# First layer's attention: casts of turned weights and turns of rows later in the lists, one root for four blocks, sums in other bursts

## The chip, the cores and the metric

The program runs on one core of a Trainium2 chip. Its engines work side by side, each from a queue of its own that it takes in order: TensorE (PE: products of matrices; its loads of the stationary operand are listed as PEld), VectorE (DVE), ScalarE (ACT), GpSimd (POOL) and SyncE (SP), from which most transfers (DMA) are issued. Semaphores hold an instruction back until what it needs is there. The metric is the time of one execution in microseconds (us); for the kernel before it is the median of three runs.

## The reference, cut to what matters

A trunk of two layers over 512 positions of width 2048, in float32. The first layer is differential attention with eight heads, the second a forgetting attention with sixteen. The change is in the first:

```python
def block(args):                       # 128 queries
    sc = jnp.einsum('bqhcd,bkhcd->bhcqk', qb, k).astype(f32) + bias[None, :, None]
    sc = jnp.where(dist >= 0, sc, NEG)
    p = jax.nn.softmax(sc, axis=-1)
    a = p[:, :, 0] - lam * p[:, :, 1]
    return jnp.einsum('bhqk,bkhe->bqhe', a.astype(v.dtype), v)
o = rms_norm(o, subln_g) * (1.0 - lam_init)
o = o.reshape(B, S, A_WIDTH) * jax.nn.silu(g)
return o @ w_out
```

Each head has two pairs of query and key (width 128), one value and one gate (width 256). Beside this, every layer needs rows of modulation, `c_act @ w_mod[l] + b_mod[l]`: a vector times a matrix of 2048 rows.

## The kernel before, in words

**Products.** Every float32 operand is split in a high part (rounded, by ACT) and a low part (the difference, by DVE), and a product is three products of parts: `products` (L172) issues L174, L175 and L176. A projection is a `group` (L303): four banks of PSUM, one per block of 128, gather sixteen slices of the contraction, two per sub-block. What PE does for one bank and one sub-block, six products, is a burst; a group has 32 of them, numbered from 0. The banks of a group are the same four as those of the group before, so burst 0 of the next group waits until bank 0 has been evacuated, burst 3 until bank 3 has. Weights come through `WeightStream` (L51): SP issues the reads (L47) three sub-blocks ahead into four stages, ACT rounds (L94) and DVE makes the low part (L95) two sub-blocks ahead of PE.

**Lists.** After each burst `tick` (L287) takes one entry of a list `pieces`: a small piece of another task, several pieces, or nothing. Then it runs `bg` steps of a background task. So the entries are places in time, one burst apart. From what is issued in this order a planner makes each engine's queue; where it reckons that an operation is not ready yet it may put a later one ahead. The operations of the background sums are kept in program order.

**Heads.** For heads h = 3 to 7 (L932) there are two groups: `qk[h]`, queries and keys, and `vg[h]`, value and gate. Beside them runs the attention of head h-1: the list `first` beside `qk[h]` (after four entries of nothing, or of the evacuation of head 2), and `rest` beside `vg[h]`. Both groups empty their list before the first evacuation. The evacuation `evac_qk` (L670) rounds (ACT) and makes the low part (DVE, L677 for queries). `evac_vg` (L683) splits v (L169, L170), takes a tanh of the gate (L694) and multiplies (sg, L695). Attention of heads 0, 1 and 7 goes by other lists, `steps` (L864); heads 0 and 1 beside `qk[2]` and `vg[2]`, head 7 beside the first group of the output projection.

**One head by blocks i = 0 to 3 of 128 queries.** `score(i, c)` multiplies (sc), takes the minimum (L723), the exponential (ACT, L727), and for the second of the pair mixes both (L731 to L735). `turn_small(i)` transposes 32 by 32 on DVE and writes to DRAM; `send(i)` issues four transfers that bring it back turned (L767); `take(i)` casts it to high and low parts (ah L777, al L778). `values(i)` multiplies with v (o). After blocks 1 and 3 `norm(p)` (L796) handles the pair p: ACT copies o to `og` and sums the squares (L804); DVE scales (L805), finds the inverse root by `rsqrt` (L242; twelve small operations, L247 to L249 and three rounds of L254 to L256), and multiplies two blocks by root and gate (L808). `turn_og(p)` transposes the rows (L821) and writes them to DRAM (L825), and `fetch` brings them back turned as `ogT` (L833).

**Pools.** `kpool` has sixteen tiles of 128 x 512. It holds the heads' turned rows (two per head) until the output projection's operands are made of them, in the bursts of `vg[7]` (`split_og`, L902: ogs L909, hh L913, hl L914).

**Sums.** `mod_stream` (L354) makes the rows of modulation in the background: DVE multiplies a slice of 128 rows and 512 columns by its part of c and adds (macc, L391). A read (L367) brings two slices, and there are two buffers (`ms`). After sixteen slices the sum is turned, reduced and put through PE (L419, L420, L429). `bg` says after which bursts a step is made: in `qk[h]` by `k % 3 > 0`, in `vg[h]` by `k % 4 > 0`, in the first group of the output projection after every burst, until none is left.

Of the kernel before, what the change touches and what calls it, by code (L numbers as in the profile page):

```python
# [10 lines left out]
F32 = mybir.dt.float32  # L11
F32R = mybir.dt.float32r
I32 = mybir.dt.int32
AF = mybir.ActivationFunctionType
ALU = mybir.AluOpType

P = 128
D = 2048
KT = D // P
T = 512  # L20
TB = T // P
A_HEADS = 8
B_HEADS = 16
NEG = -1e30
EPS = 1e-5
# [85 lines left out]
def tile_yoco(  # L111
# [24 lines left out]
    V, S, PE, G = nc.vector, nc.scalar, nc.tensor, nc.gpsimd  # L136
# [8 lines left out]
    kpool = ctx.enter_context(tc.tile_pool(name="kpool", bufs=16))  # L145
# [95 lines left out]

    def rsqrt(y, v, n, pool):  # L242

        t = pool.tile([P, n], I32, name="rs_t", tag=f"rs_t{n}", bufs=2)
        a = pool.tile([P, n], F32, name="rs_a", tag=f"rs_a{n}", bufs=2)
        h = pool.tile([P, n], F32, name="rs_h", tag=f"rs_h{n}", bufs=2)
        V.tensor_scalar(t, v.bitcast(I32), 1, None, op0=ALU.logical_shift_right)  # L247
        V.tensor_scalar(y.bitcast(I32), t, -1.0, float(0x5F3759DF), op0=ALU.mult, op1=ALU.add)
        V.tensor_scalar(h, v, -0.5, None, op0=ALU.mult)  # L249
        for _ in range(3):  # L250
            if n == 1:
                V.scalar_tensor_tensor(a, y, h, y, op0=ALU.mult, op1=ALU.mult)
            else:
                V.tensor_tensor(a, y, y, op=ALU.mult)  # L254
                V.tensor_tensor(a, a, h, op=ALU.mult)
            V.scalar_tensor_tensor(y, a, 1.5, y, op0=ALU.add, op1=ALU.mult)  # L256
# [182 lines left out]
    with tc.tile_pool(name="start", bufs=2, reuse_waits="tile") as sp, tc.manual_schedule(engines={ET.DVE}):  # L439
# [154 lines left out]
        def turn():  # L594
            lower()
            columns()
            while sum(sets[at["set"] - 1]) <= at["kt"]:
                sums()
                columns()
            turned.append((at["kt"], turn_x(at["kt"])))  # L600
            at["kt"] += 1
# [66 lines left out]
    cur = {}  # L668
# [29 lines left out]
    fetches = {}  # L698

    def attention_a(h, lead=3, late=(), spread=False):  # L700
# [37 lines left out]
        def turn(i):  # L738
            def fn():
                w = (i + 1) * P  # L740
                pt = tr_bank()
                a = st["e", i, 0]
                for j in range(i + 1):
                    PE.transpose(pt[:, j * P : (j + 1) * P], a[:, j * P : (j + 1) * P], ident)
                ah = ap.tile([P, 512], F32R, name="ah", tag="ah")
                al = ap.tile([P, 512], F32R, name="al", tag="al")
                split(ah[:, :w], al[:, :w], pt[:, :w])
                st["a", i] = (ah, al)
            return fn
# [32 lines left out]
        def values(i):  # L782
            def fn():
                if i % 2 == 0:
                    st["o", i // 2] = o_bank()
                o = st["o", i // 2][:, (i % 2) * 256 : (i % 2 + 1) * 256]
                ah, al = st["a", i]
                vh, vl = cur[h, "v"]
                for j in range(i + 1):
                    js = slice(j * P, (j + 1) * P)  # L790
                    products(o, (ah[:, js], al[:, js]), (vh[:, j, :], vl[:, j, :]), j == 0, j == i)
                if i % 2 == 1:
                    norm(i // 2)
            return fn

        def norm(p):  # L796
            o = st["o", p]
            og = ap.tile([P, 2, 256], F32, name="og", tag="og", bufs=1)
            ss = ap.tile([P, 2], F32, name="ss", tag="ss", bufs=2)
            rstd = ap.tile([P, 2], F32, name="rstd", tag="rstd", bufs=2)  # L800
            S.copy(og.rearrange("p r e -> p (r e)"), o)
            for r in range(2):
                orow = o[:, r * 256 : (r + 1) * 256]
                S.activation(orow, orow, AF.Square, accum_out=ss[:, r : r + 1])  # L804
            V.tensor_scalar(ss, ss, 1.0 / 256.0, EPS, op0=ALU.mult, op1=ALU.add)  # L805
            rsqrt(rstd, ss, 2, ap)
            for r in range(2):
                V.scalar_tensor_tensor(  # L808
                    og[:, r, :], og[:, r, :], rstd[:, r : r + 1], cur[h, "sg"][:, 2 * p + r, :],
                    op0=ALU.mult, op1=ALU.mult,  # L810
                )
            st["og", p] = og

        def turn_og(p):
            def fn():
                if p == 0:
                    st["turned"] = dram.tile([P, TB * 256], F32, name="turned_og", tag="turned_og", bufs=2)
                t = ap.tile([P, 512], F32, name="tog", tag="tog", bufs=1)  # L820
                V.transpose(  # L821
                    t.rearrange("p (b r c) -> p r b c", r=2, c=32), st["og", p].rearrange("p r (b c) -> p r b c", c=32)
                )
                to = st["turned"].rearrange("p (b t c) -> p b t c", t=TB, c=32)[:, :, 2 * p : 2 * p + 2, :]
                nc.sync.dma_start(to, t.rearrange("p (b r c) -> p b r c", r=2, c=32))  # L825
            return fn
# [23 lines left out]
        if spread:  # L850
            r, d, k = ([part(i) for i in range(TB)] for part in (turn_small, send, take))
            first = [
                score(0, 0), None, score(0, 1), None, [score(1, 0), r[0]], None, [score(1, 1), d[0]], None, [k[0], r[1]], None,
                [score(2, 0), d[1]], values(0), k[1], None, score(2, 1), None, [values(1), r[2]], score(3, 0), d[2], None, k[2],
                score(3, 1),
            ]
            rest = [
                values(2), r[3], turn_og(0), d[3], None, k[3], None, None, None, values(3), *[None] * 9, turn_og(1), None, None,
                None, fetch,
            ]  # L860
            if h == 2:
                first[9] = fetches[1]
            return first, rest
        steps = [  # L864
            *[None] * lead, score(0, 0), *late[0:1], score(0, 1), *late[1:2], score(1, 0), *late[2:3], score(1, 1), *late[3:4],
# [6 lines left out]
        if h == A_HEADS - 1:  # L872
# [1 line left out]
                values(2), store(0), turn(3), store(1), values(3), None, None, None, None, store(2), store(3),  # L874
            ]
        return steps + [
            values(2), turn_og(0), turn(3), None, values(3), None, None, None, None, turn_og(1), None,
        ]

    def drain():  # L880
# [51 lines left out]
    for h in range(3, A_HEADS):  # L932

        first_steps, rest = attention_a(h - 1, spread=True)
        if h == 3:
            pieces.extend(lambda b=b: evac_qk(2)(b, raw["qk", b]) for b in range(4))
            late = first_vg(2, raw)
            for n in range(4):
                first_steps[2 * n + 1] = late[n]
        else:  # L940
            pieces.extend([None] * 4)
        pieces.extend(first_steps)

        def evac(b, acc, h=h):
            if b == 0:
                drain()
            evac_qk(h)(b, acc)

        group(qk[h], False, evac, bg=lambda k: k % 3 > 0)
        pieces.extend(rest)  # L950

        def evac_rest(b, acc, h=h):
            if b == 0:
                drain()
            evac_vg(h)(b, acc)

        def early(s):
            if s >= 1:
                split_og((2 * s - 2, 2 * s - 1))

        group(vg[h], True, evac_rest, bg=lambda k: k % 4 > 0, after_sub=early if h == A_HEADS - 1 else None)

    def ktile(name):
        return kpool.tile([P, T], F32, name=name, tag="K")
# [14 lines left out]
    def out_projection(jobs, layer, zp, opened, residual, norm, after_held=None):  # L979


        ready = {}

        def prepare(k):
            if k < len(jobs):
                ready[k] = residual(jobs[k][0], jobs[k][2])

        prepare(0)
        for k, (f, job, banks) in enumerate(jobs):
            if layer == 1:  # L990

                pieces.extend([None] * (8 if k else 0) + [lambda k=k: prepare(k + 1)])
            elif k:
                prepare(k)
            res = ready[k]
            gate = ktile("gate")
            row_bcast(gate, gate_dram[layer][0, 512 * f : 512 * (f + 1)])

            def evac(b, acc, f=f, res=res, gate=gate):
                if f == 0 and b == 0:  # L1000
                    drain()
                    opened()
                pool, z, stats = zp
                zs = z[:, b, 512 * f : 512 * (f + 1)]
                tmp = pool.tile([P, 512], F32, name="ztmp", tag="htmp", bufs=2)
                V.tensor_tensor(tmp, acc, gate, op=ALU.mult)
                res(b, zs, tmp)
                V.bn_stats(stats[:, b, f, :], zs)
                if f == 3:
                    norm(b)  # L1010

            last = k == len(jobs) - 1
            group(job, True, evac, banks, bg=1 if k == 0 and layer == 0 else 0, hold=(5, 6)[layer] if last else 0, after_held=after_held if last else None)

    nctx = ExitStack()
    zp = []
# [475 lines left out]
```

## Time and profile before

| what | before |
|---|---|
| median of 3 runs | 1970.86 us (1968.74 to 1971.88) |
| the profiled execution | 1972.9 us, of it 1970.8 in its span |
| PE busy | 1928.8 us, 98% |
| PEld busy | 1596.6 us, 81% |
| DVE busy | 1351.6 us, 69% |
| ACT busy | 695.6 us, 35% |
| granted clock of PE, mean | 0.994 |

The groups of the first layer lie, by the trace, between about 180 and 816 us; the output projection follows. In a row of the timeline stand the start (us), the duration, the engine, the line, the operation, what is written and read, and in brackets the idle time of the engine ahead of it with what ended that. A row of waits gives who waited for whom, the total, how often, and the longest. A row of windows gives for a stretch of time what each engine was busy for, the granted clock, the DMA engines' share and their rate. PE's products are pipelined, so that the next starts before the one ahead has ended as drawn.

### The profile page before, as it was taken

What the parts mean: (1) busy time and instruction counts of PE and PEld (TensorE: products, weight loads), DVE (VectorE), ACT (ScalarE), POOL (GpSimd) and SP (SyncE); (2) the same over time, 40 slices, a digit from 0 to 9 for tenths busy, and PEclk for the clock granted to TensorE, in tenths of its full rate; (3) what the DMA queues carried; (4) which work ended last, traced back from release to release, by engine and by line L of the source; (5) the groups of instructions that cost most, each with busy time, mean ns of one, the idle gap of its engine ahead of it and who ended that gap; (6) DMA issues with size and microseconds to landing.
All of it is one profiled execution on the core that took longest, in us unless ns stands there. A gap on an engine that the chain in (4) does not pass through costs nothing.

```text
span 1970.8 us, 25187 instructions
## 1 busy us (share of the span) xinstructions
PE 1928.8 (98%) x8833; PEld 1596.6 (81%) x8833; DVE 1351.6 (69%) x2494; ACT 695.6 (35%) x1175; POOL 2.2 (0%) x10
## 2 busy tenths in 40 slices
PE   5999999999999999999999999999999999999997
PEld 4888888788888878788888888888888888888886
DVE  7885678777777778853475665666466666676657
ACT  2432444323333334431264222224344344353123
POOL 0000000000000000000000000000000000000000
PEclk8999999999999999999999999999999999999999
DMA  9983455777777777753345765664355555553622
GB/s 343 356 306 111 129 177 168 233 228 221 248 229 241 225 242 222 235 169 97 108 160 193 261 230 193 224 219 134 110 149 152 156 152 158 148 172 114 229 88 106
DMA packets 336378, 376.11 MB, mean 191 GB/s; under 512 B 69334, under 2 KB 238316, under 8 KB 335484
## 3 DMA queue, kind: packets, MB, share of 16 engines
q1 hardware_dynamic: 333872, 370.30, 59.3%
q10 hardware_dynamic: 2380, 4.21, 0.6%
q8 instruction: 69, 1.13, 0.2%
q14 instruction: 57, 0.47, 0.1%
HBM read 345.63 MB, written 28.79 MB: 190 GB/s over the span
## 4 chain that ended last, share of the span: by engine, by line
PE 83%; DVE 8%; DMA 6%; issue 1%; SPq 1%; ACT 1%; DVEq 0%; ACTq 0%
PE acc L174 24%; PE acc L175 24%; PE acc L176 24%; DMA ms<-in_w_mod_dram 2%; DVE macc L391 2%; DMA ms<-in_kv_w_mod_dram 2%; PE sc L174 2%; PE sc L175 2%; PE sc L176 2%; PE o L174 1%; DVE wlo L95 1%; PE o L176 1%; PE o L175 1%; SPq L471 1%; DMA sms<-in_w_mod_dram 1%
## 5 line engine op out<-in xcount | busy, mean ns | idle before, releaser
L95 DVE TENSOR_TENSOR wlo<-wst,whi 128x1024 fp32r<-128x1024 f32 (+2 forms) x322 | 384.3, 1195 | 338.7 <-ACT whi L94 329.4
L94 ACT CAST whi<-wst 128x1024 fp32r<-128x1024 f32 (+2 forms) x322 | 331.6, 1031 | 755.9 <-PE acc L176 361.8
L174 PE MATMUL acc<-whi,hh 128*128 128x512 f32 x1232 | 482.5, 395 | 5.3 <-DVE sg L695 2.4
L175 PE MATMUL acc<-wlo,hh 128*128 128x512 f32 x1232 | 480.9, 390 | 0.3 <-DVE wlo L95 0.3
L176 PE MATMUL acc<-whi,hl 128*128 128x512 f32 x1232 | 480.5, 390 | 0.0
L174 PE MATMUL acc<-hh,whi 128*128 128x512 f32 x1184 | 463.5, 391 | 1.2 <-DVE sg L695 1.1
L175 PE MATMUL acc<-hl,whi 128*128 128x512 f32 x1184 | 461.6, 390 | 0.0
L176 PE MATMUL acc<-hh,wlo 128*128 128x512 f32 x1184 | 461.2, 389 | 0.0
L174 PEld LDWEIGHTS acc<-whi,hh 128*128 128x128 f32 x1232 | 232.7, 189 | 54.3 <-issue 4.6
L176 PEld LDWEIGHTS acc<-whi,hl 128*128 128x128 f32 x1232 | 231.7, 188 | 48.6
L175 PEld LDWEIGHTS acc<-wlo,hh 128*128 128x128 f32 x1232 | 231.9, 188 | 46.4 <-DVE wlo L95 0.7
L176 PEld LDWEIGHTS acc<-hh,wlo 128*128 128x128 f32 x1184 | 222.3, 188 | 47.5
L174 PEld LDWEIGHTS acc<-hh,whi 128*128 128x128 f32 x1184 | 222.5, 188 | 45.3 <-issue 1.9
L175 PEld LDWEIGHTS acc<-hl,whi 128*128 128x128 f32 x1184 | 222.6, 188 | 42.0
L391 DVE SCALAR_TENSOR_TENSOR macc<-ms,cact,macc 128x512 f32<-128x512 f32 x300 | 223.7, 746 | 42.5 <-DMA ms<-in_kv_w_mod_dram 24.7
L498 DVE SCALAR_TENSOR_TENSOR sacc<-sms,cact,sacc 128x512 f32<-128x512 f32 (+1 forms) x127 | 89.5, 705 | 4.8 <-DMA sms<-in_w_mod_dram 1.2
L727 ACT ACTIVATE e<-e,mn 128x128 f32<-128x128 f32 (+3 forms) x64 | 36.0, 563 | 112.1 <-DVE mn L723 108.5
L1298 ACT ACTIVATE eb<-eb,mnb 128x128 f32<-128x128 f32 (+1 forms) x64 | 36.0, 563 | 89.1 <-DVE mnb L1295 88.9
L1295 DVE CUSTOM_DVE_ANT_0 eb<-sc,biasb 128x128 f32<-128x128 f32 (+1 forms) x64 | 31.1, 486 | 22.4 <-PE sc L176 21.6
L391 DVE SCALAR_TENSOR_TENSOR macc<-msk,cact,macc 128x512 f32<-128x512 f32 x60 | 45.0, 750 | 1.4
L723 DVE CUSTOM_DVE_ANT_0 e<-sc,bias 128x128 f32<-128x128 f32 (+3 forms) x64 | 30.9, 484 | 16.7 <-PE sc L176 16.5
L1289 DVE SCALAR_TENSOR_TENSOR biasb<-nfb,F,mask 128x128 f32<-128x128 f32 (+1 forms) x64 | 34.7, 543 | 0.6
(270 smaller groups left out, 1734.3 us busy)
## 6 DMA issues: line engine op xcount, KB each, us to landing
wst<-in_a_w_in_dram SPq DMA_DIRECT2D x240, 256.0 KB, 4.1
ms<-in_w_mod_dram SPq DMA_DIRECT2D x64, 512.0 KB, 4.4
ms<-in_kv_w_mod_dram SPq DMA_DIRECT2D x64, 512.0 KB, 4.7
wst<-in_kv_w_dram SPq DMA_DIRECT2D x64, 512.0 KB, 3.8
wst<-in_b_w_in_dram SPq DMA_DIRECT2D x128, 256.0 KB, 3.0
sms<-in_w_mod_dram SPq DMA_DIRECT2D x56, 512.0 KB, 6.8
wst<-in_a_w_out_dram SPq DMA_DIRECT2D x32, 512.0 KB, 3.8
msk<-in_w_mod_dram SPq DMA_DIRECT2D x64, 256.0 KB, 5.8
```

Source lines behind the costliest of these rows:

```text
L94: self.nc.scalar.copy(hi[:, :, :w], st[:, :, :w])
L95: self.nc.vector.tensor_tensor(lo[:, :, :w], st[:, :, :w], hi[:, :, :w].bitcast(F32), op=ALU.subtract)
L174: PE.matmul(dst, lhs[0], rhs[0], start=start, stop=False)
L175: PE.matmul(dst, lhs[0], rhs[1], start=False, stop=False)
L176: PE.matmul(dst, lhs[1], rhs[0], start=False, stop=stop)
L391: ins = V.scalar_tensor_tensor(acc, w, cact[:, kt : kt + 1], acc, op0=ALU.mult, op1=ALU.add)
L498: V.scalar_tensor_tensor(acc, w, sc, acc, op0=ALU.mult, op1=ALU.add)
L723: V.tensor_tensor_reduce(out=e[:, :w], in0=sc[:, :w], in1=st["bias"][:, (3 - i) * P :], scale=-1.0, scalar=3.0e38, op0=ALU.add, op1=ALU.mi ...
L727: S.activation(e[:, :w], e[:, :w], AF.Exp, bias=mn, scale=-1.0, accum_out=rs)
L1289: V.scalar_tensor_tensor(bias[:, :w], cur[hd, "nf"][:, :w], F[:, i, hd : hd + 1], mask[:, (3 - i) * P :], op0=ALU.add, op1=ALU.add)
L1295: V.tensor_tensor_reduce(out=e[:, :w], in0=sc[:, :w], in1=bias[:, :w], scale=-1.0, scalar=3.0e38, op0=ALU.add, op1=ALU.min, accum_out=mn)
L1298: S.activation(e[:, :w], e[:, :w], AF.Exp, bias=mn, scale=-1.0, accum_out=rs)
```

## The change

Four things, all in the first layer's attention:

- *Lists.* In `first` the casts of blocks 0, 1 and 2 stand one entry later (from 8, 12 and 20 to 9, 13 and 21). In `rest` the cast of block 3 goes from entry 5 to 7, the value products of block 3 from 9 to 11, the turn of the first two blocks' rows from 2 to 17; the turn of the other two stays at 19 and the fetch at 23. In the lists of heads 0 and 1 the first turn of rows goes next to the second.
- *One root.* For all heads but the last, `norm(0)` only copies and sums the squares, into a tile of four columns; `norm(1)` finds the root of four columns at once and scales all four blocks. The second pair's copy and its turned rows lie in tiles of `kpool`. The last head keeps a root for each pair.
- *Sums.* In `qk[h]` steps follow bursts under 26 that leave less than 4 on division by 5 (21 steps, as before). In `vg[h]` they follow bursts under 28 that are no multiple of 7 (24 steps, as before); in `vg[7]` the bound is 24 (20 steps). In the first group of the output projection they begin after burst 4.
- *Tiles of `rsqrt`.* They are four columns wide whatever is asked for, and are cut to it.

```diff
     def rsqrt(y, v, n, pool):
 
-        t = pool.tile([P, n], I32, name="rs_t", tag=f"rs_t{n}", bufs=2)
-        a = pool.tile([P, n], F32, name="rs_a", tag=f"rs_a{n}", bufs=2)
-        h = pool.tile([P, n], F32, name="rs_h", tag=f"rs_h{n}", bufs=2)
+        t, a, h = (pool.tile([P, 4], d, name=k, tag=k, bufs=2)[:, :n] for k, d in (("rs_t", I32), ("rs_a", F32), ("rs_h", F32)))
...
+        halves = h == A_HEADS - 1
+
         def norm(p):
             o = st["o", p]
-            og = ap.tile([P, 2, 256], F32, name="og", tag="og", bufs=1)
-            ss = ap.tile([P, 2], F32, name="ss", tag="ss", bufs=2)
-            rstd = ap.tile([P, 2], F32, name="rstd", tag="rstd", bufs=2)
+            if p == 0 or halves:
+                og = ap.tile([P, 2, 256], F32, name="og", tag="og", bufs=1)
+                st["ss"] = ap.tile([P, 4], F32, name="ss", tag="ss", bufs=2)
+            else:
+                og = kpool.tile([P, T], F32, name="og", tag="K").rearrange("p (r e) -> p r e", r=2)
+            ss = st["ss"]
+            c0 = 0 if halves else 2 * p
             S.copy(og.rearrange("p r e -> p (r e)"), o)
             for r in range(2):
                 orow = o[:, r * 256 : (r + 1) * 256]
-                S.activation(orow, orow, AF.Square, accum_out=ss[:, r : r + 1])
-            V.tensor_scalar(ss, ss, 1.0 / 256.0, EPS, op0=ALU.mult, op1=ALU.add)
-            rsqrt(rstd, ss, 2, ap)
-            for r in range(2):
+                S.activation(orow, orow, AF.Square, accum_out=ss[:, c0 + r : c0 + r + 1])
+            st["og", p] = og
+            if p == 0 and not halves:
+                return
+            rstd = ap.tile([P, 4], F32, name="rstd", tag="rstd", bufs=2)
+            n = c0 + 2
+            V.tensor_scalar(ss[:, :n], ss[:, :n], 1.0 / 256.0, EPS, op0=ALU.mult, op1=ALU.add)
+            rsqrt(rstd[:, :n], ss[:, :n], n, ap)
+            for k in range(n):
+                q, c = (p, k) if halves else (k // 2, k)
+                row = st["og", q][:, k % 2, :]
                 V.scalar_tensor_tensor(
-                    og[:, r, :], og[:, r, :], rstd[:, r : r + 1], cur[h, "sg"][:, 2 * p + r, :],
-                    op0=ALU.mult, op1=ALU.mult,
+                    row, row, rstd[:, c : c + 1], cur[h, "sg"][:, 2 * q + k % 2, :], op0=ALU.mult, op1=ALU.mult
                 )
-            st["og", p] = og
...
-                t = ap.tile([P, 512], F32, name="tog", tag="tog", bufs=1)
+                if p:
+                    t = kpool.tile([P, T], F32, name="tog", tag="K")
+                else:
+                    t = ap.tile([P, 512], F32, name="tog", tag="tog", bufs=1)
...
             first = [
-                score(0, 0), None, score(0, 1), None, [score(1, 0), r[0]], None, [score(1, 1), d[0]], None, [k[0], r[1]], None,
-                [score(2, 0), d[1]], values(0), k[1], None, score(2, 1), None, [values(1), r[2]], score(3, 0), d[2], None, k[2],
-                score(3, 1),
+                score(0, 0), None, score(0, 1), None, [score(1, 0), r[0]], None, [score(1, 1), d[0]], None, r[1], [k[0]],
+                [score(2, 0), d[1]], values(0), None, k[1], score(2, 1), None, [values(1), r[2]], score(3, 0), d[2], None, None,
+                [score(3, 1), k[2]],
             ]
             rest = [
-                values(2), r[3], turn_og(0), d[3], None, k[3], None, None, None, values(3), *[None] * 9, turn_og(1), None, None,
-                None, fetch,
+                values(2), r[3], None, d[3], None, None, None, k[3], None, None, None, values(3), *[None] * 5, turn_og(0), None,
+                turn_og(1), None, None, None, fetch,
             ]
             if h == 2:
-                first[9] = fetches[1]
+                first[9].append(fetches[1])
...
-            values(2), turn_og(0), turn(3), None, values(3), None, None, None, None, turn_og(1), None,
+            values(2), None, turn(3), None, values(3), None, None, None, None, turn_og(0), turn_og(1),
...
-        group(qk[h], False, evac, bg=lambda k: k % 3 > 0)
+        group(qk[h], False, evac, bg=lambda k: 1 if k < 26 and k % 5 < 4 else 0)
...
-        group(vg[h], True, evac_rest, bg=lambda k: k % 4 > 0, after_sub=early if h == A_HEADS - 1 else None)
+        group(vg[h], True, evac_rest, bg=lambda k, n=28 if h < A_HEADS - 1 else 24: 1 if k < n and k % 7 else 0, after_sub=early if h == A_HEADS - 1 else None)
...
-            group(job, True, evac, banks, bg=1 if k == 0 and layer == 0 else 0, hold=(5, 6)[layer] if last else 0, after_held=after_held if last else None)
+            group(job, True, evac, banks, bg=(lambda n: 1 if n > 3 else 0) if k == 0 and layer == 0 else 0, hold=(5, 6)[layer] if last else 0, after_held=after_held if last else None)
```

## The prediction

> **What bounds the kernel now.** I read the page's first part first, then the waits of PE over the stage that the change touches (180 to 900 us), then the timeline around each of those waits, and last the windows of DVE.
>
> ```profile
> span 1970.8 us, 25187 instructions
> PE 1928.8 (98%) x8833; PEld 1596.6 (81%) x8833; DVE 1351.6 (69%) x2494; ACT 695.6 (35%) x1175; POOL 2.2 (0%) x10
> ```
>
> PE is busy for 98% and the change leaves its products alone, so only time in which PE waits can be won. PE's waits in the stage:
>
> ```profile
> PE acc L174 <- DVE sg L695: 3.5, 3, 2.4
> PE acc L174 <- DVE q0l L677: 1.8, 3, 0.8
> PE o L174 <- ACT ah L777: 1.7, 1, 1.7
> PE tr L429 <- DVE mred L420: 0.4, 1, 0.4
> PE tr L744 <- DVE e L735: 0.2, 1, 0.2
> ```
>
> Columns: total us, times, longest. That is 7.6 us in nine waits. Each costs a little more than it shows:
>
> ```profile
> 572.06 0.39 PE L176 MATMUL acc<-hh,wlo 128*128 128x512 f32 x1
> 573.29 0.47 PE L174 MATMUL acc<-whi,hh 128*128 128x512 f32 x1 [0.84 <-DVE q0l L677]
> ```
>
> In the dense stream one product starts about 0.23 us after the other (a burst of six takes 1.36 us), but is drawn 0.39 us long. So 0.16 us of each wait is hidden: here 1.23 - 0.23 = 1.00 us is lost, not 0.84. One wait has a sequel in the granted clock:
>
> ```profile
> 391.34 0.39 PE L176 MATMUL acc<-whi,hl 128*128 128x512 f32 x1
> 393.40 0.39 PE L174 MATMUL o<-vh,ah 128*128 128x256 f32 x1 [1.67 <-ACT ah L777]
> ```
>
> ```profile
> 391.61:395.03 3.42, 1.75 (x11) 1.32 (x11) 1.61 (x3) 0.62 (x1) 0.00 (x0) 1.00 0.92 315
> 395.03:398.44 3.41, 3.41 (x12) 2.83 (x11) 2.00 (x8) 1.53 (x5) 0.00 (x0) 0.50 0.52 153
> ```
>
> (Length; busy PE, PEld, DVE, ACT, POOL; clock; DMA share; GB/s.) PE is busy for half of a 3.42 us stretch, and the next 3.41 us run at clock 0.50, which costs half of them, 1.7 us. Ceiling of the whole change: 7.6 + 9 x 0.16 + 1.7 = 10.7 us, 0.5% of the time.
>
> **The change part by part.** *Head 2's values (3.5 us).* The transpose for block 3 and its four sends stay at entries 1 and 3 of the second list; the cast goes from entry 5 to 7 and the value products from 9 to 11. PE arrives two bursts, 2.7 us, later, and missed the cast by 2.06 - 0.23 = 1.83 us. What is late next is the read back from DRAM itself, with 0.9 us to spare. Gain 1.83 + 1.7 = 3.5 us; between 0 (the read slips as far) and 3.5 I take all, as the send keeps its place.
>
> *Ends of the q/k projections (2.3 us).* The first evacuation of the next bank needs the low part of q0 from DVE, whose queue reads:
>
> ```profile
> 567.01 0.88 DVE L808 SCALAR_TENSOR_TENSOR og<-og,rstd,sg 128x256 f32<-128x256 f32 x2
> 568.27 0.70 DVE L821 STREAM_TRANSPOSE tog<-og 128x512 f32<-128x512 f32 x1
> 569.53 0.74 DVE L391 SCALAR_TENSOR_TENSOR macc<-ms,cact,macc 128x512 f32<-128x512 f32 x1
> 570.19 1.22 DVE L95 TENSOR_TENSOR wlo<-wst,whi 128x1024 fp32r<-128x1024 f32 x1
> 571.80 0.74 DVE L391 SCALAR_TENSOR_TENSOR macc<-ms,cact,macc 128x512 f32<-128x512 f32 x1
> 572.46 0.68 DVE L677 SCALAR_TENSOR_TENSOR q0l<-acc,q0h 128x512 fp32r<-128x512 f32 x1
> ```
>
> Of these the scaling of the first two blocks (0.88), their transpose (0.70) and one of the two sums (0.66 from start to start) leave the place, since blocks 0 and 1 wait for one root with 2 and 3, and sums stop at burst 26. That is 2.2 us against 1.0 lost. Gain: 1.8 + 3 x 0.16 = 2.3 us; ends 0 and 2.3, and I take all. Late next would be the weights' low part, still two sub-blocks ahead.
>
> *End of the last v/gate projection (2.5 us).*
>
> ```profile
> 816.14 0.47 PE L174 MATMUL acc<-whi,hh 128*128 128x512 f32 x1 [2.38 <-DVE sg L695]
> ```
>
> ```profile
> 808.58 1.54 DVE L391 SCALAR_TENSOR_TENSOR macc<-ms,cact,macc 128x512 f32<-128x512 f32 x2 [2.18 <-DMA ms<-in_w_mod_dram]
> 810.04 1.89 DVE L914 TENSOR_TENSOR hl<-ogs,hh 128x512 fp32r<-128x512 f32 x3
> 813.58 0.75 DVE L391 SCALAR_TENSOR_TENSOR macc<-ms,cact,macc 128x512 f32<-128x512 f32 x1
> 814.24 0.42 DVE L170 TENSOR_TENSOR vl<-acc,vh 128x256 fp32r<-128x256 f32 x1
> ```
>
> DVE stands 2.18 us before a sum whose rows have not landed, with three low parts queued behind it, then the v split. The change runs no sum from burst 24 on: the 2.18 us and three sums ahead of the split (2.0 us) go. Gain 2.38 + 0.16 = 2.5 us; the floor is 0, I take all.
>
> *Ends of the other v/gate projections (1.4 us, taken at 0.7).* The two other waits on sg have 3.5 - 2.4 = 1.1 us and 0.3 hidden. No sum runs in the last four bursts (three did), but the next list has one after each of its bursts 0, 1 and 2 (two did). Between 0 and 1.4 I take half.
>
> *The sums' new density.* A v/gate projection does its 24 sums in 28 bursts, not 32: six of seven, one per 1.59 us where it was 1.81. Two sums share a read, and two reads are out:
>
> ```profile
> DVE macc L391: 36.7, 37
> DMA to landing us min/median/max: 3.6/4.5/6.3
> ```
>
> (Waits of sums on reads, 376 to 816 us.) A buffer's turn is then four sums' time, 4 x 1.59 = 6.4 us, against a median read of 4.5 and two sums of 0.75, together 6.0: just enough, and with reads at 6.3 it is not. DVE will stand more often. Its room in a v/gate projection, in the last one, and in the output projection after it:
>
> ```profile
> 475.80:523.00 47.20, 46.69 (x216) 38.69 (x215) 36.73 (x62) 12.46 (x20) 0.00 (x0) 1.00 0.83 251
> 768.00:800.00 32.00, 32.00 (x153) 26.91 (x152) 28.10 (x51) 11.70 (x20) 0.00 (x0) 1.00 0.78 238
> 816.00:836.00 20.00, 19.51 (x93) 15.98 (x94) 18.43 (x47) 7.66 (x21) 0.00 (x0) 1.00 0.74 251
> ```
>
> 10.5 us in 47 idle covers it; if that cover is gone the v split at a projection's end is late again, at most 1.0 us at each of five ends (the largest seen). Cost between 0 and 5 us; I take 0.7, as 37 such waits today cost PE only the few above.
>
> *Output projection.* The first group of it has nine sums after bursts 4 to 12, beside the last head's scores, where it had five after 0 to 4: 4 x 0.66 = 2.7 us more in a stretch where DVE is busy for 18.4 of 20 us and PE waits for 0.5. From 0 to 2.7; I take 0.8.
>
> *One root for four blocks.* Thirteen small operations (some 0.16 us each) go per head; two scalings and a transpose come to the v/gate part:
>
> ```profile
> L808 DVE SCALAR_TENSOR_TENSOR og<-og,rstd,sg 128x256 f32<-128x256 f32 x20 | 8.8, 482 | 0.2
> L255 DVE TENSOR_TENSOR rs_a<-rs_a,rs_h 128x2 f32<-128x2 f32 x30 | 4.8, 159 | 0.7
> ```
>
> There 2 x 0.48 + 0.70 = 1.7 us come; 2.1 go from the head. The turned rows are written some 2 us later, ahead of a fetch four entries on; on SP's queue what stands behind that write is weight reads three sub-blocks ahead (some 16 us), so nothing. The extra tiles from the pool of sixteen: at most twelve are held by turned rows then. The moved turns of rows in heads 0 and 1 have a whole projection until their fetch. The casts' later entries spare ACT some of its standing before a read (4.04 us in a row quoted below), for which PE has not waited outside head 2. The turn of blocks 0 and 1 takes its write out of SP's queue ahead of the sends, which helps head 2 at most; POOL's queue carries nothing of this. Wider tiles in the other roots change no operation. All at nothing.
>
> **Sum.** 3.5 + 2.3 + 2.5 + 0.7 - 0.7 - 0.8 = 7.5 us. The profiled execution took 1972.9 us (1970.8 in its span), 2 us over the median of three, 1970.86: I expect 1965.4 for such a one and 1963.4 us as median.
>
> **The rivals.**
> *Reads cannot keep up.* If reads land near 6 us under the denser traffic (DMA share 0.83 already), DVE stands before most sums and the v/gate ends stay late, the last too. Against the forecast 2.5 + 0.7 go and 2.5 more is lost: gain 1.8 us, 1969.1. For it speak the 37 waits; against it the four to eight bursts left to catch up. Chance 0.20.
>
> *Casts too near their values (slower).* The casts for blocks 0 and 1 go one burst nearer to their products.
>
> ```profile
> 450.11 0.30 ACT L777 CAST ah<-e 128x128 fp32r<-128x128 f32 x1 [4.04 <-DMA e<-turned]
> 450.44 0.29 DVE L778 TENSOR_TENSOR al<-e,ah 128x128 fp32r<-128x128 f32 x1 [1.88 <-ACT ah L777]
> 451.00 0.28 PE L174 MATMUL o<-vh,ah 128*128 128x256 f32 x1
> ```
>
> The slack is 0.27 us here. Were each of ten casts a burst later, PE would lose about 1.1 at each, 11 us, less 7.5: 3.5 us slower, 1974.4. It decides from 0.75 us a cast on. Against it: the cast waits for the read, not for its place, and the send has not moved. Chance 0.13.
>
> *The moves have no hold.* An operation runs where the planner finds it ready, not where the list has it. Then head 2's wait stays and the gain is 4.0 us: 1966.9. The two sends' distance to PE speaks against it. Chance 0.10.
>
> *The slow stretch stays.* If the clock's fall at 395 us came from something else than that wait, 1.7 us stay: gain 5.8, 1965.1. [...] Chance 0.07. [...]
>
> **How the numbers follow.** Forecast 0.50, rivals 0.20, 0.13, 0.10, 0.07. The least that can be told from no change is about 0.2%, 3.9 us. Faster: 0.50 + 0.07 + half of "no hold" (it lies at the bound) = 0.62; same 0.20 + 0.05 = 0.25; slower 0.13. Low end: all of the ceiling but 0.5 is 10.2 us, and a median 1.2 lower by scatter: 1959.5. The high end takes in the reads that cannot keep up, and scatter: 1972. For the forecast alone 1960 to 1967.
>
> **What would show it.** In the profile after, PE's waits on the cast and on q0l are gone and no clock of 0.50 stands in the stage (steps 1, 2); the wait on sg at the first output projection is gone, with no sum before the v split (step 3); waits of sums on reads are more and longer. Wrong it would be if waits on the casts of blocks 0 and 1, or on a sum's read at a projection's end, stand among PE's, or if DVE's windows at the v/gate ends are full.

## The result, and the profile after

| | before | after |
|---|---|---|
| median of 14 runs each | 1968.98 us (1965.37 to 1971.88) | 1972.86 us (1970.04 to 1976.11) |
| ratio, with its 95% interval | | 1.0022 (1.0013 to 1.003) |
| profiled execution, its span | 1972.9, 1970.8 | 1976.11, 1974.3 |

The change costs about 4.3 us by the ratio (3.9 between the medians); a gain of 7.5 was forecast. The page after, first part:

```profile
span 1974.3 us, 25066 instructions
PE 1928.9 (98%) x8833; PEld 1596.5 (81%) x8833; DVE 1343.7 (68%) x2403; ACT 694.0 (35%) x1175; POOL 2.2 (0%) x10
```

PE's work is the same to 0.1 us, and DVE's is 7.9 us less: 91 instructions, the small operations of the roots, are gone. PE's waits from 180 to 900 us, after:

```profile
PE acc L174 <- DVE sg L693: 4.0, 5, 1.9
PE tr L427 <- DVE mred L418: 2.5, 2, 1.7
PE o L174 <- ACT ah L775: 1.6, 2, 1.1
PE acc L174 <- ACT whi L94: 1.0, 1, 1.0
PE acc L174 <- ACT raw L908: 0.9, 1, 0.9
PE o L176 <- DVE al L776: 0.3, 1, 0.3
```

The waits on q0l are gone, as said. But sg, the reduced row (mred), the casts, a weight's high part and a raw copy are there: 10.3 us in twelve waits, where 7.6 in nine stood before. The dearest, with what follows it, is the longer one on mred, in the first group of the output projection. Timeline of PE, then its windows:

```profile
847.95 0.39 PE L175 MATMUL acc<-wlo,hh 128*128 128x512 f32 x1
850.03 0.27 PE L427 MATMUL tr<-fours,mred 128*64 128x32 f32 x2 [1.69 <-DVE mred L418]
```

```profile
847.86:851.27 3.41, 1.72 (x11) 1.11 (x10) 2.21 (x4) 0.05 (x1) 0.00 (x0) 1.00 0.18 61
851.27:854.68 3.41, 3.41 (x12) 2.72 (x11) 0.41 (x1) 1.60 (x4) 0.00 (x0) 0.50 0.65 190
```

PE stands for 1.69 us and then runs 3.41 us at clock 0.50. Why mred is late is in DVE's timeline ahead of it:

```profile
846.15 0.74 DVE L389 SCALAR_TENSOR_TENSOR macc<-ms,cact,macc 128x512 f32<-128x512 f32 x1
846.82 0.74 DVE L733 SCALAR_TENSOR_TENSOR e<-e,rsum 128x512 f32<-128x512 f32 x1
847.48 0.70 DVE L417 STREAM_TRANSPOSE mturn<-macc 128x512 f32<-128x512 f32 x1
848.11 1.18 DVE L95 TENSOR_TENSOR wlo<-wst,whi 128x1024 fp32r<-128x1024 f32 x1
849.21 0.67 DVE L418 TENSOR_REDUCE mred<-mturn 128x16 f32<-128x512 f32 x1
```

The last sums now fall among the last head's scores, and the product of the reduced row is due one burst after the reduction is issued. Where the time was lost shows in the start of the first product on the weights that the output projection holds for its last bursts (tile `held`, before and after; each row gives the first and the last start):

```profile
L174 PE MATMUL acc<-held,hh x48: 388/389/477, 977.7 to 1958.0; 128*128 128x512 f32 x48
```

```profile
L174 PE MATMUL acc<-held,hh x48: 387/389/477, 980.6 to 1960.8; 128*128 128x512 f32 x48
```

2.9 us are lost by 980.6. At the start of the last v/gate group the changed kernel was 0.4 us ahead (766.30 against 766.67), so in these two profiles 3.3 us go in that group and the output projection after it. The profile before is of a long execution, though. A second one, shown below, is at these two places at 762.69 and 973.5 us; against it 3.6 us are lost ahead of the last v/gate group and 3.5 in it and behind.

### The profile page after: what moved, and what is told of

The parts are those of the page before. It is cut to its first block, busy times and chain, and to the rows that moved or that the text cites. A ratio compares the mean times of both kernels' runs of the same rounds, so it can differ in the third digit from the quotient of the medians.

```text
span 1974.3 us, 25066 instructions
## 1 busy us (share of the span) xinstructions
PE 1928.9 (98%) x8833; PEld 1596.5 (81%) x8833; DVE 1343.7 (68%) x2403; ACT 694.0 (35%) x1175; POOL 2.2 (0%) x10
## 4 chain that ended last, share of the span: by engine, by line
PE 81%; DVE 8%; DMA 6%; issue 2%; SPq 1%; ACT 1%; DVEq 0%; ACTq 0%
PE acc L174 24%; PE acc L175 24%; PE acc L176 24%; DVE macc L389 2%; DMA ms<-in_kv_w_mod_dram 2%; DVE wlo L95 2%; PE sc L175 2%; PE sc L176 2%; PE sc L174 2%; DMA ms<-in_w_mod_dram 1%; PE o L174 1%; PE o L176 1%; PE o L175 1%; DMA sms<-in_w_mod_dram 1%; SPq L469 1%
```

## The experiments

Ratios are to the kernel before, run beside it on the same chip, with 95% intervals; 0.001 is 2.0 us.

**The sums undone, and the sums alone.**

```diff
# sums_back, against after
-        group(qk[h], False, evac, bg=lambda k: 1 if k < 26 and k % 5 < 4 else 0)
+        group(qk[h], False, evac, bg=lambda k: k % 3 > 0)
...
-        group(vg[h], ..., bg=lambda k, n=28 if h < A_HEADS - 1 else 24: 1 if k < n and k % 7 else 0, ...)
+        group(vg[h], ..., bg=lambda k: k % 4 > 0, ...)
...
-            group(job, ..., bg=(lambda n: 1 if n > 3 else 0) if k == 0 and layer == 0 else 0, ...)
+            group(job, ..., bg=1 if k == 0 and layer == 0 else 0, ...)
```

> The changed kernel with the background sums after the bursts of the kernel before (all three groups); the lists, the one root and the tiles stay changed. Theory S (the sums' places cost: they are one per 1.59 us in the v/gate groups and pile up on the output projection's first group): the 1.69 us wait of PE on the last row's reduction and the half clock behind it (3.4 us together) go, the value products of heads 2 and 6 no longer wait (1.1 and 0.5 us), and what the lists gained at head 2 (3.5 us) stays: ratio to the kernel before 0.997 to 0.999. Theory L (the moved lists and the one root reorder the queues and cost by themselves): the ratio stays at 1.001 to 1.003.

Measured: 0.9997 (0.9988 to 1.0006).

`sums_only` makes the reverse edit in the kernel before.

> The kernel before with the sums' new places alone. Theory S: the waits of the changed kernel on the last row's reduction and at the v/gate ends appear, and the wait of 1.67 us on head 2's cast with its half clock stays: ratio 1.002 to 1.005. Theory L: the ends of the q/k groups are freed and nothing is lost: ratio 0.997 to 1.000.

Measured: 1.0017 (1.0008 to 1.0026). The two bracket the change: the sums' places cost 0.0017 alone and 0.0025 inside it, and lists and root together are worth nothing that can be measured. Theory S stands by the side on which both fall, though both lie just outside the ranges that it gave: the lists' 3.5 us are not there, and in the profile of `sums_only` the wait on head 2's cast for block 3, which was to stay, is not there either.

**The casts alone, and the root alone.**

```diff
# casts_only, against before: first as in the change, and
-                values(2), r[3], turn_og(0), d[3], None, k[3], None, None, None, values(3), *[None] * 9, turn_og(1), None, None,
-                None, fetch,
+                values(2), r[3], turn_og(0), d[3], None, None, None, k[3], None, None, None, values(3), *[None] * 7,
+                turn_og(1), None, None, None, fetch,
```

> The kernel before with the casts and the last value products later in the lists, the turns of rows, two roots and the sums as before. Both theories: the wait of PE on head 2's cast for block 3 goes, with the half clock (3.5 us): ratio 0.998. Theory L in the form that the casts' entries reorder ACT's queue: new waits on the value products, ratio 1.000 to 1.002.

Measured: 0.9988 (0.9977 to 1.0000). PE's waits in this profile:

```profile
PE acc L174 <- DVE sg L695: 2.6, 1, 2.6
PE tr L744 <- DVE e L735: 0.2, 1, 0.2
```

The wait on the cast is gone, and so are those on q0l, with the sums and the root as before. The wait of 2.6 us on sg is followed by a stretch at clock 0.50 (from 807.16 us).

`root_only` has the change's `norm` and tiles, with `turn_og(0)` and `turn_og(1)` at entries 17 and 19, on the casts and sums of before.

> The kernel before with one root for four blocks and the turns of rows next to each other late in the lists; casts, value products and sums as before. If it is neutral or gains by DVE's shorter work ahead of q0l: ratio 0.998 to 0.9995, the waits on q0l gone. If its chain holds up the raw copies at the third group's end as in the changed kernel (0.9 us on raw): ratio 1.000 to 1.001.

Measured: 0.9998 (0.9988 to 1.0008). No wait on q0l, but 0.9 us on the raw copy and waits on sg of up to 3.4 us: neutral. The longest of these (522.79 us) is followed by a stretch at clock 0.50.

**The kernel before, once more.**

> The kernel before, unchanged, for a second profile. If head 2's wait of 1.67 us on ah and the half clock behind it belong to the kernel, both are seen again; if they were chance, this profile lacks them and its span is 2 to 4 us shorter than 1970.8.

Measured: a span of 1966.4 us, with no clock below 1.00 in the stage.

```profile
392.32 0.39 PE L174 MATMUL o<-vh,ah 128*128 128x256 f32 x1 [1.10 <-ACT ah L777]
```

Head 2's wait is there again, with 1.10 us for 1.67; the half clock is not. Nor is the wait in every kernel with the old entries: `dense_vg` below has 0.78 us of it, `root_only` none. The waits on q0l, 1.8 us in three in the first profile, are one of 0.2 us here; those on sg are 3.4 us in three as before, and a second wait on a cast (0.85 us, at 553 us) is new. The profile on which the prediction was built was of an execution 3.9 us over the median of fourteen.

**The sums by parts.** `dense_vg` gives the v/gate groups of heads 3 to 6 their new places, `tail_only` the last v/gate group and the output projection, `qk_only` the q/k groups; each on the kernel before.

> The kernel before with one part of the sums' new places alone: in the v/gate groups of heads 3 to 6 the 24 sums follow six of seven bursts and stop at 28. Theory R (the reads cannot keep up, so sums queue to the end of the group): waits of PE on sg or on the weights' parts at those ends stay or grow, ratio 1.0005 to 1.0015. Theory T (the loss lies in the tail: last v/gate group and output projection): ratio 0.999 to 1.000, the two waits of 1.1 us on sg at those ends gone.

Measured: 1.0007 (0.9998 to 1.0016); 5.0 us of waits on sg in four. Not decided, and no gain.

> The kernel before with the tail alone: the last v/gate group without sums from burst 24 and the output projection's sums from burst 4. Theory T: the wait of 2.38 us on sg shrinks, but the last row's reduction comes among the last head's scores and PE waits for it 1 to 2 us, at times with a half clock: ratio 1.0005 to 1.002. Theory R: the wait on sg goes and nothing comes for it: ratio 0.9985 to 0.9995.

Measured: 1.0000 (0.9991 to 1.0009); a wait on sg of 2.6 us is still there. It lies between the two theories: nothing won and nothing lost. The wait is followed by a stretch at clock 0.50 (from 810.25 us), as 2.38 us at that place in the kernel before were not (clock 1.00).

```diff
# qk_only, against before
-        group(qk[h], False, evac, bg=lambda k: k % 3 > 0)
+        group(qk[h], False, evac, bg=lambda k: 1 if k < 26 and k % 5 < 4 else 0)
```

> The kernel before with the q/k groups' sums alone changed (four of five bursts under 26). Both theories: the three waits of 1.8 us on q0l at those groups' ends go, ratio 0.9985 to 0.9995. If the denser start of the group delays head 2's scores and casts instead, ratio 1.000 to 1.001 with waits of PE on ah.

Measured: 1.0025 (1.0015 to 1.0035). The part that was to be a sure gain costs 4.9 us by itself, outside both of the ranges expected. It is also more than `sums_only` (1.0017), which holds it, though the two intervals overlap: the parts do not simply add. PE's waits in the stage are 2.6 us on ah in two, 2.1 on sg in two and 1.2 on q0l in two. Its PE, at head 6's first value products, and the window after that wait:

```profile
739.81 0.39 PE L174 MATMUL o<-vh,ah 128*128 128x256 f32 x1 [1.99 <-ACT ah L777]
```

```profile
741.35:744.76 3.41, 3.41 (x10) 2.65 (x9) 1.28 (x2) 0.00 (x0) 0.00 (x0) 0.51 0.93 298
```

In this profile the whole loss lies here: `qk_only` starts the last q/k group at 712.99 us, the second profile of the kernel before at 713.28, and at the end of the slow stretch it is 3.6 us behind (the same product at 746.39 and 742.78).

Twelve us before the wait its DVE stood before a sum, with the score's mixing (L731) behind it:

```profile
728.24 0.75 DVE L391 SCALAR_TENSOR_TENSOR macc<-ms,cact,macc 128x512 f32<-128x512 f32 x1 [0.95 <-DMA ms<-in_w_mod_dram]
728.91 0.16 DVE L731 RECIPROCAL rsum<-rsum 128x2 f32<-128x2 f32 x1
...
730.63 0.31 DVE L757 STREAM_TRANSPOSE e<-e 128x128 f32<-128x128 f32 x1
```

Counted from the group's first product (712.99 here, 716.40 before), the mixing starts 0.8 us later than before, the four sends 1.7 us later, and the cast 3.3 us later. The last 1.6 us come on ACT:

```profile
737.55 0.75 DVE L391 SCALAR_TENSOR_TENSOR macc<-ms,cact,macc 128x512 f32<-128x512 f32 x1 [1.03 <-DMA ms<-in_w_mod_dram]
738.22 0.55 DVE L723 CUSTOM_DVE_ANT_0 e<-sc,bias 128x384 f32<-128x384 f32 x1
738.86 0.62 ACT L727 ACTIVATE e<-e,mn 128x384 f32<-128x384 f32 x1 [5.37 <-DVE mn L723]
739.48 0.28 ACT L777 CAST ah<-e 128x128 fp32r<-128x128 f32 x1
```

The cast of block 0 runs behind an exponential of block 2, whose minimum was behind another sum that stood before its read. In the kernel before the cast came first (739.62, the exponential 740.95). From the group's first product to this cast DVE stood before sums for 2.6 us in four pieces; in the two profiles of the kernel before it was 0.4 and 1.0, in one piece each. Head 6 had 1.25 us to spare between its low part and the products (740.24 to 741.49 before), head 3 only 0.27.

**Is it the reads?** `qk_noread` is `qk_only` with the sums' reads left out but for two; `qk_traffic` sends the reads it no longer needs to a place in DRAM.

```diff
# qk_noread, against qk_only (qk_traffic adds the two lines marked T)
+            if nk > 1 and k > 1:
+                loaded[k] = kept[k % 2]
T                away = dram.tile([P, 2, 512], F32, name="away", tag="away", bufs=2)
T                nc.sync.dma_start(away, rows.rearrange("(k p) n -> p k n", p=P))
+                return
```

> The kernel with the q/k groups' sums alone changed, with the reads of the first layer's background sums left out but for the first two: the sums run on those two tiles again and again, so the rows of modulation are other numbers. If the reads are what makes the denser sums cost (a sum standing before its read ahead of the scores on DVE, and the heads' turned rows landing late behind the reads): the waits of PE on ah (2.0 us at head 6, 0.5 at head 2) go, ratio 0.995 to 0.998. If DVE's own time is what lacks, the waits stay and the ratio is 1.001 to 1.003.

Measured: 0.9958 (0.9943 to 0.9973). All that is left of PE's waits in the stage:

```profile
PE tr L748 <- DVE e L739: 0.2, 1, 0.2
```

> The kernel with the q/k groups' sums alone changed, its sums on the first two tiles again and again (so the rows of modulation are other numbers), and the reads it no longer needs sent from the weights to a place in DRAM: the reads' traffic stays, no sum waits for one. If the loss comes from sums that stand on DVE before their read with the scores, the casts and the evacuations behind them: ratio 0.995 to 0.997, as without reads, no wait on ah or sg above 0.5 us. If it comes from the traffic ahead of the heads' own transfers: waits on ah of 1 us or more stay, ratio 0.999 or above.

Measured: 0.9963 (0.9951 to 0.9974), again one wait of 0.2 us. All three kernels issue the same sums after the same bursts, and with no read to wait for they cost PE nothing: DVE's time for the sums themselves was not what was short. Whether it was the waiting for reads or their traffic is settled for the first part of the stage alone. Windows of `qk_only`, then of `qk_traffic`:

```profile
336.00:550.00 214.00, 213.02 (x985) 177.28 (x984) 170.79 (x347) 68.06 (x130) 0.00 (x0) 1.00 0.79 240
550.00:816.00 266.00, 260.63 (x1189) 214.71 (x1189) 210.15 (x420) 99.78 (x183) 0.00 (x0) 0.99 0.75 228
```

```profile
336.00:550.00 214.00, 213.92 (x990) 178.08 (x989) 171.33 (x353) 70.61 (x134) 0.00 (x0) 1.00 0.81 254
550.00:816.00 266.00, 266.00 (x1231) 221.38 (x1230) 218.99 (x445) 104.70 (x193) 0.00 (x0) 1.00 0.40 119
```

The reads without a buffer to wait for ran ahead: the last was issued at 538 us. Up to 550 us `qk_traffic` moves more than `qk_only` (254 GB/s for 240) and PE waits for nothing, so there traffic alone costs PE nothing. Behind that it moves 119 GB/s for 228, as `qk_noread` does (120), and there lie 5.3 of the 6.4 us of PE's waits in `qk_only`, head 6's among them. For these, traffic is not excluded by a run; head 6's rows speak for the standing.

Two more things change together with DVE's standing. SP, too, stands before a sum's read until its buffer is free, with the heads' transfers and the weights' reads behind it (between 336 and 816 us, for sums at L391 that still use the buffer: 100.0 us before, 82.3 in `qk_only`, none in `qk_traffic`). At head 6 this adds little: the write of the turned rows is issued 1.0 us later than before, when the mixing alone is 0.8 later. And the order on ACT is the planner's: in `qk_traffic` head 6's cast again runs ahead of the exponential (730.11 and 732.94). How much of the loss is the new order and how much the standing itself, no run here parts.

**Inside the whole change.** `qk_back` is the changed kernel with the q/k groups' sums as before.

> The changed kernel with the q/k groups' sums alone as before. If their density is the largest part of the loss: ratio to the kernel before 0.9995 to 1.0005, down from 1.0022. If the parts do not add up this way (the v/gate groups' density or the tail carry the loss inside the whole change): 1.0015 or above.

Measured: 1.0008 (0.9997 to 1.0018): by these figures 1.4 of the 2.2 per mille come from these groups (the two intervals overlap), and about 0.001 is left open between the other sums. PE's waits in its profile are 6.1 us in seven for 10.3 in twelve, none of them on a cast; the largest item is mred, 3.5 us in two. `late_pe` puts five more steps between the last reduction and its product, in the changed kernel:

```diff
-        for _ in summed[0]:
-            yield
+        for _ in summed[0]:
+            for _ in range(6 if nk > 1 else 1):
+                yield
```

> The changed kernel with five more steps between the reduction of the last row of the first layer's background sums and its product on PE; nothing else. If that product's wait (1.69 us, then 3.4 us at half clock) is what turns the change into a loss, the output projection's start falls by 3.5 us: ratio to the kernel before 1.0005, half a per mille from no change. If the wait only moves (to the transposes of the last head behind it), the ratio stays at 1.002.

Measured: 1.0013 (1.0004 to 1.0022). 0.9 per mille, 1.8 us, for 3.4 expected; the intervals of the two overlap. The tail's wait on mred, with its half clock, was a large item of one profile; in the median it seems a smaller one. Waits on the casts are 4.1 us in four in this profile, for 1.6 in two in the changed kernel's, though the edit does not touch them.

**Better versions.** `best1` has the later casts and moves six sums from the last eight bursts of `vg[7]` to the q/k group of head 2.

```diff
# best1, against casts_only
-group(qk[2], ..., bg=lambda k: k % 3 == 2)
+group(qk[2], ..., bg=lambda k: k % 2)
...
-        group(vg[h], ..., bg=lambda k: k % 4 > 0, ...)
+        group(vg[h], ..., bg=(lambda k: k % 4 > 0) if h < A_HEADS - 1 else (lambda k: k < 24 and k % 4 > 0), ...)
```

> The casts and the last value products later in the lists, as in the kernel with casts alone; beside it six sums are moved from the last eight bursts of the last v/gate group to the q/k group of head 2 (every second burst instead of every third), so that the output projection has no more of them than before. If the last group's wait on sg (2.6 us with casts alone) comes from a sum that stands before its read: that wait goes, ratio 0.997 to 0.998. If DVE is late there for the heads' low parts alone, the wait stays at 1 us or more, ratio 0.9985.

Measured: 0.9979 (0.997 to 0.9988), with 1.2 us left of the wait on sg. So a part of that wait stays when no sum runs near it: in `best1` the last one ahead of it ends at 801.2 us, and the heads' and the weights' low parts are late there by themselves. The interval overlaps that of `casts_only`.

`best2` also ends the other q/k groups' sums at burst 26 with their old density (`k < 26 and k % 3 > 0`); the twenty left out go to `qk[2]` (every burst) and `vg[2]`.

> The kernel with the casts later and six sums moved to head 2's q/k group, and beside that the sums of the other q/k groups stop at burst 26 without becoming denser (two of three as before); the twenty that this leaves out go to the two groups ahead of head 3, so that the last row falls where it did. If the stop at 26 gains and only the density costs: the waits on q0l are gone, ratio 0.996 to 0.9975. If the two early groups have no room for them: ratio 0.998 to 1.000 with new waits of PE there.

Measured: 0.9969 (0.9957 to 0.9980). The waits on q0l are gone and 1.8 us on e has come in the early groups. `best3` spreads the moved sums over both (`k % 5 > 0` in each).

> As the kernel with the q/k groups' sums stopped at 26, but the sums moved ahead are spread over both early groups (25 of 32 bursts in each); two go to the output projection. If the 1.8 us wait of PE on e and the 2.6 us lost by the third group's end come from the first early group being filled to every burst: both shrink, ratio 0.9955 to 0.9965. Otherwise as that one, 0.997.

Measured: 0.9970 (0.9959 to 0.9982): the wait on e shrinks to 0.6 us, one on sg of 1.5 is there, the time is the same. Both intervals overlap that of `best1`. These two beat the kernel before by some 6 us and the changed one by 10. So the change's own idea, with the sums moved to where little waits behind them, is worth a gain here.

## Why the prediction was wrong

- **Ends of the q/k projections: the step that failed.** It put 2.3 us of gain on what leaves DVE's queue ahead of q0l and nothing on the sums' density there; the step on density looked at the v/gate groups alone. 21 sums in 26 bursts are four more than the 17 that stood there, beside scores and casts whose value products had 0.27 to 1.35 us to spare. Alone, this part costs 4.9 us (1.0025); inside the whole change it is some 2.8 us (`qk_back`), with a wide margin. The gain itself was small besides: the waits on q0l, 1.8 us in the profile that was read, are 0.2 in the second profile of the same kernel, and 1.2 are left when these sums alone are changed. That they are gone in the changed kernel shows little, as they are gone in `casts_only` and `root_only` too.
- **Casts too near their values.** The rival had the right side, and its price of 3.5 us slower came near 4.3, but by luck. It has ten casts late by 1.1 us each, for their entries; the changed kernel shows two late casts (1.6 us together) and no half clock behind them, and `casts_only`, with these entries, is not slower (0.9988). Where a cast is late, a sum stood before its read ahead of the score: at head 6 in `qk_only`, and in the changed kernel at head 2, where a sum at 341.61 us stood for 1.44 with the mixing of block 0 behind it and PE waited 1.07 us for the cast.
- **Reads cannot keep up.** That the reads are needed for the loss is right (`qk_noread`). That they would be slower is not: they land in 4.4 us by the median where it was 4.5, and DVE stands before fewer sums and a little longer at each (38.8 us in 32, where it was 36.7 in 37): of the prediction's own sign, "more and longer", half is there. The total hardly grew; where DVE stands is what matters.

```profile
  DVE macc L389: 38.8, 32
DMA to landing us min/median/max: 3.5/4.4/6.2
```

- **End of the last v/gate projection.** 2.5 us were taken as sure, since no sum is issued from burst 24 on. But sums issued by then were still queued. The 247th sum is the last that is issued in this group, by burst 23 and so by some 799 us (766.30 and 24 bursts of 1.36); in the changed kernel's DVE it runs 12 us later:

```profile
811.24 0.75 DVE L389 SCALAR_TENSOR_TENSOR macc<-ms,cact,macc 128x512 f32<-128x512 f32 x1 [2.89 <-DMA ms<-in_w_mod_dram]
811.91 1.22 DVE L95 TENSOR_TENSOR wlo<-wst,whi 128x1024 fp32r<-128x1024 f32 x1
```

  PE then waits on sg for 1.86 us and for 0.76 more. `tail_only` says 1.0000. `best1`, which takes sums out of the group, brings the wait to 1.2 us and not to nothing.
- **Head 2's values.** The step was right in kind, as no kernel with the new entries has the wait (most variants with the old ones have none either), and too large: 3.5 us for a wait that in the second profile was 1.10 (1.26 with the hidden part) and had no half clock behind it. The casts alone gave 2.4 us (0 to 4.5).
- **The sum's base.** Half clock and wait were read from one execution, 2 us over the three runs shown and 3.9 over the fourteen; the gain was taken off the median all the same. By the second profile, which has no half clock in the stage, that took some 1.7 us too much (an estimate: half of the 3.41 us at clock 0.50).
- **Ends of the other v/gate projections, density there.** Put at +0.7 and -0.7; measured together 1.0007 (0.9998 to 1.0016), a loss of 1.4 us that may be nothing.
- **Output projection.** Taken at 0.8 of at most 2.7 us; what it did not see is that the last reduction would come behind them with its product one burst later. `late_pe` puts 1.8 us on it.
- **One root.** At nothing, and neutral (`root_only`). PE's waits in its profile are on sg and on a raw copy instead of q0l, but waits of this kind also differ between the two profiles of the kernel before.
- **The slow stretch stays.** It did not stay: in the changed kernel the clock is 1.00 there, and the one stretch at 0.50 in the stage follows another wait, of 1.69 us for 1.67. In the second profile of the kernel before, with 1.10 us of wait at head 2, no clock below 1.00 is in the stage. In these profiles, then, the stretch went with the wait, and the rival falls. That such a wait always brings it is not shown: the last section has longer ones with a clock of 1.00 behind them.

## What to carry to other kernels

Background work that waits for its own reads should not be put ahead of a short chain on an engine that takes its queue in order, as DVE at head 6 of `qk_only` (0.95 us before one sum, 1.03 before another, the scores' operations behind them): count how many such operations stand in the new place, not only how many leave the old one, and hold them against the smallest slack of what is queued behind. That an operation is issued by a certain point says nothing of when it runs: for the 247th sum 12 us lay between. A wait that one profile shows can be all but gone in a second one of the same kernel, as those on q0l were (1.8 and 0.2 us); take both before a gain of half a per cent is added up.

## What the runs showed of the hardware

After some of PE's waits the granted clock was 0.50 for 3.41 us, after others as long it was 1.00; the profiles of both kernels have one of each:

| profile | PE waits | the wait ends at | granted clock after it |
|---|---|---|---|
| before | 1.67 us on ah | 393.40 us | 0.50 from 395.03 to 398.44 us |
| before | 2.38 us on sg | 816.14 us | 1.00 up to 1960 us |
| after | 1.86 us on sg | 814.47 us | 1.00 up to 850.03 us |
| after | 1.69 us on mred | 850.03 us | 0.50 from 851.27 to 854.68 us |
| `qk_only` | 1.99 us on ah | 739.81 us | 0.51 from 741.35 to 744.76 us |

Between 100 and 1960 us neither the profile before nor the one after shows another stretch below 1.00. `casts_only`, `root_only` and `tail_only` have one behind waits of 2.6, 3.4 and 2.6 us. In the second profile of the kernel before, with waits on sg of up to 2.2 us, no clock below 1.00 is in the stage. The mean granted clock is 0.994 in the six profiles named here with such a stretch, and 0.995 or 0.996 in the other eleven.

So behind 1.67, 1.69 and 1.99 us of waiting another 1.7 us were lost (an estimate: half of 3.41 us), behind 1.86 and 2.38 us none by the clock. The length of the wait alone does not tell the one from the other; what does was not shown.
